# The low part of every third block of weights: a negated copy and an accumulating DMA in place of a subtraction

## The chip, the cores and the metric

The kernel runs on one NeuronCore of one Trainium2 chip. The metric is the device time of one execution in microseconds (us). The engines are named TensorE (PE; its weight loads are PEld), VectorE (DVE), ScalarE (ACT), GpSimd (POOL) and SyncE (SP).

## The reference

One layer of a decoder trunk for 256 tokens of width 2048, in float32. The input is RMS-normalised and multiplied by one wide matrix, `w_in`. From its columns come four attention mixers (sparse with an indexer, forgetting, differential, dilated), each with four heads, and their gates. Each mixer's output is projected by `w_branch` and merged, and the sum is projected by `w_out`.

```python
h = rms_norm(x, norm_w)
p = h @ w_in
...
for b in range(N_BRANCHES):
    y = branches[b].reshape(bsz, seq, BRANCH_WIDTH).astype(x.dtype) * jax.nn.silu(z_parts[b])
    term = jax.nn.sigmoid(g_parts[b]) * (y @ w_branch[b])
    merged = term if merged is None else merged + term
return (x + merged @ w_out).astype(x.dtype)
```

The final output is one more RMS norm. Nearly all of the work is in the matrix products with the three weight matrices, about 177 MB of weights, each of which is read once.

## The kernel before, in words

**Products in two parts.** TensorE multiplies in a reduced float32 format (`F32R`). To keep float32 accuracy each operand is split in two: the high part is the value rounded to that format, and the low part is the value minus the high part. A product is the sum of three: high by high, high by low, low by high. The activations are split once; the weights are split as they come.

**Units.** The weights are cut into 169 units (class `Unit`). A unit is mostly four chunks of 128 rows by 512 columns, 1024 KB, and the products that use it. There are two forms. In a [column, token] unit (`T_units`, for q, k and the gate path z) the weights are the stationary operand: for each of 16 blocks there is one product with the high part (line 278, 512 columns of tokens in two parts) and one with the low part (line 283, 256 columns). In a [token, column] unit (`tok_units`, for v, the gates, `w_branch` and `w_out`) the activations are stationary and the weights stream: 24 products per unit, in triples (lines 273, 274, 275), of which the third streams the low part. The order of the units is written out at the end of `body`: the indexer's 8 units and a small one, then for each of the four mixers 16 units for q, k, z and v, 16 for gates and 4 for `w_branch`, and at the end 16 for `w_out`.

**Load and split.** `load` (line 118) brings a unit's weights to a tile `raw` by a DMA issued from SP; there are 4 such tiles. `split` has ScalarE copy `raw` to the high part `whi` (line 134) and VectorE subtract that from `raw` into the low part `wlo` (line 135). `whi` and `wlo` have three buffers each (`SPLIT + 1`), used in turn. The main loop (line 839) issues for unit i: the split of unit i+2, the load of unit i+6, the products of unit i, the evictions of its results (`post`), and then one step of each active thread (attention heads and other small work, which use all engines). The engines run their own instructions in this order. So the split of unit i+2 writes the buffers that unit i-1 has read.

**Other work on the queues.** GpSimd does the scaling by 1/rms of q, k and z (lines 334, 345), the merge's additions (line 658), small operations of the differential mixer (lines 605, 606), and a few DMAs, among them the loads of `xf` and `fw` for the end (lines 670, 672). ScalarE does half of the evictions, the exponentials and the sigmoids. SP issues only the loads and, at the end, the stores.

Of the kernel before, what the change touches and what calls it, by code (L numbers as in the profile page):

```python
# [11 lines left out]
F32 = mybir.dt.float32  # L12
F32R = mybir.dt.float32r
AF = mybir.ActivationFunctionType
ALU = mybir.AluOpType

P = 128
# [35 lines left out]
def shape_constants():  # L53
    """Rows: one-hot T5 bucket of each distance, causal mask, dilated multiplicity."""
    oh = np.zeros((NBUCKETS + 2, VLEN), np.float32)
    for i in range(VLEN):
        d = i - 127
        if d < 0:
            oh[NBUCKETS:, i] = NEG
            continue  # L60
        oh[bucket(d), i] = 1.0
        mult = int(d <= 128) + int(d % 4 == 0) + int(d % 16 == 0)
        oh[NBUCKETS + 1, i] = math.log(mult) if mult else NEG
    co = np.zeros((NBUCKETS + 2, 13), np.float32)
    co[NBUCKETS, 0:8] = 1.0
    co[NBUCKETS, 12] = 1.0
    co[NBUCKETS + 1, 8:12] = 1.0
    return oh, co


class Unit:
    """A block of weights (nk chunks of 128 rows by n columns) and the products that use it."""

    def __init__(self, src, k0, nk, c0, n, mm, post=(), need=(), start=()):
        self.src, self.k0, self.nk, self.c0, self.n = src, k0, nk, c0, n
        self.mm, self.post = mm, list(post)
        self.need, self.start = list(need), list(start)


@with_exitstack  # L80
def body(ctx: ExitStack, tc, x, norm_w, w_in, fox_b_f, lq1, lk1, lq2, lk2, subln_w,
         w_branch, w_out, rel_bias, final_w, oh, co, out):
    nc = tc.nc
    x = x[0]
# [20 lines left out]

# [1 line left out]
    def load(u, parts=1, part=None):  # L107
# [14 lines left out]
    def split(u, hi=None, lo=None, parts=1, part=None):  # L122
        if not part:
            if hi is None:
                hi = wp.tile([P, 2048], F32R, name="whi", tag="whi", bufs=SPLIT + 1)
                lo = wp.tile([P, 2048], F32R, name="wlo", tag="wlo", bufs=SPLIT + 1)
            n_ = u.nk * u.n
            u.hi = hi[:, :n_].rearrange("p (k n) -> p k n", k=u.nk)
            u.lo = lo[:, :n_].rearrange("p (k n) -> p k n", k=u.nk)
        step = u.nk // parts  # L130
        raw = u.raw[:, :u.nk * u.n].rearrange("p (k n) -> p k n", k=u.nk)
        for i in range(0, u.nk, step) if part is None else (part * step,):
            s_ = slice(i, i + step)
            nc.scalar.activation(u.hi[:, s_], raw[:, s_], AF.Copy)  # L134
            nc.vector.tensor_tensor(u.lo[:, s_], raw[:, s_], u.hi[:, s_].bitcast(F32),  # L135
                                    op=ALU.subtract)

# [1 line left out]
    nw = const.tile([16, P], F32, name="nw")  # L139
# [29 lines left out]

# [1 line left out]
    hT = big.tile([P, KC, 2, S], F32R, name="hT", tag="r1")  # L171
# [45 lines left out]

# [1 line left out]
    bias = at.tile([P, 13, S], F32, name="bias")  # L219
# [27 lines left out]

# [1 line left out]
    def h_act(k):  # L249
        return hT[:, k, 0], hT[:, k, 1]  # L250

    def tok_units(src, c0, act, nk, evict, name, n=512, need=(), start=()):
        """[token, column] tiles, activations stationary."""
        st = {}
        units = []
        for k0 in range(0, nk, 4):
            def mm(u, k0=k0):
                if k0 == 0:
                    st["ps"] = [main_ps(name) for _ in range(2)]
                for t in range(2):  # L260
                    tok_mm(st["ps"][t][:, :n], u, act, k0, nk, t)
            units.append(Unit(src, k0, 4, c0, n, mm))
        units[0].need += need
        units[-1].post.append(lambda: evict(st["ps"]))
        units[-1].start += start
        return units
# [19 lines left out]
    def T_units(c0, evict, name, start=(), ps_of=main_ps):  # L286
        """512 columns as four [column, token] tiles; each bank holds two halves to be added."""
        st = {}
        units = []
        for k0 in range(0, KC, 4):  # L290
            def mm(u, part=None, between=None, k0=k0):
                if k0 == 0 and not part:
                    st["ps"] = [ps_of(name) for _ in range(4)]
                ps = st["ps"]
                if part is None:
                    for j in range(4):
                        for k in range(4):
                            T_hi(ps[j], u, k0, j, k)
                            T_lo(ps[j], u, k0, j, k)
                else:  # L300
                    for f in (T_hi, T_lo):
                        for k in (2 * part, 2 * part + 1):
                            for j in range(4):
                                f(ps[j], u, k0, j, k)
                            if between is not None:
                                between()
                                between = None
            units.append(Unit(w_in, k0, 4, c0, 512, mm))
        units[-1].post.append(lambda: evict(st["ps"]))
        units[-1].start += start  # L310
        return units
# [45 lines left out]

# [1 line left out]
    ki_hi = at.tile([P, S], F32R, name="ki_hi")  # L359
# [15 lines left out]
    def misc_thread():  # L375
# [9 lines left out]
        for t in range(2):  # L385
# [3 lines left out]
                                           rst[:, t:t + 1], bf_sb, op0=ALU.mult, op1=ALU.add)  # L389
        # cumulative log forget gates, as rows: log sigmoid(f) = min(f, 0) - log(1 + exp(-|f|))  # L390
        fv = fl.rearrange("p t h -> p (t h)")
# [21 lines left out]
    def fox_bias(t, h):  # L413
        """Where the first branch's biases were."""
        return bias[:, h] if t else selb[h // 2][:, (h % 2) * P:(h % 2 + 1) * P]
# [18 lines left out]
    def ev_iq(ps, i):  # L434
        """Four chunks of two heads each; a head's high and low parts stacked on the partitions."""
        qf = big.tile([P, 4, S], F32, name="qf", tag="y")
        for j in range(4):
            add_halves(qf[:, j], ps[j])
        active.append(("", stack_thread(qf, i)))
# [47 lines left out]

# [1 line left out]
    # A head's logits: columns 0:128 the first query block, 128:384 the second.  # L489
    SL = (slice(0, 128), slice(128, 384))  # L490
# [8 lines left out]
    def softmax(ps, bias_of):  # L499
        """exp(logit - max) and its sums."""  # L500
        lg = at.tile([P, 384], F32, name="lg", tag="lg", bufs=3)
# [17 lines left out]
    def transposed(pr):  # L519
        """[key, query] pieces: keys 0:128 x queries 0:256, keys 128:256 x queries 128:256."""  # L520
        tp = att_ps("ptp")
        nc.tensor.transpose(tp[:, 0:128], pr[:, 0:128], ident)
        nc.tensor.transpose(tp[:, 128:256], pr[:, 128:256], ident)
        nc.tensor.transpose(tp[:, 256:384], pr[:, 256:384], ident)
        pt = at.tile([P, 384], F32, name="pt", tag="pt", bufs=2)
        nc.scalar.activation(pt, tp[:, :384], AF.Copy)
        return pt
# [5 lines left out]
    def put_y(h, o, scale=None):  # L533
        """o: [column, token]; the branch's product with its gate path, split."""
        yT = V["yT"]
# [82 lines left out]

# [1 line left out]
    V["g"] = {}  # L620
# [41 lines left out]

# [1 line left out]
    def open_final():  # L664
# [20 lines left out]
    def partial(t):  # L685
        """All of the mean square but its last piece, and epsilon."""
        part = V["mg"].tile([P, 1], F32, name="part", tag="part", bufs=2)
# [4 lines left out]
    def final(t, n, part):  # L692
        """1 / rms times the columns (all but the last n have final_w in them)."""
        xf, fs, fw = V["xf"], V["fs"], V["fw"]
# [23 lines left out]
    def out_units(n):  # L718
        if n < 3:
# [3 lines left out]
            return tok_units(w_out, n * 512, m_act, KC, ev, "ps_o")  # L723
        # the last columns: one token block after the other, the weights kept
        st = []
# [21 lines left out]

# [1 line left out]
    def att_threads(b, fn):  # L749
# [21 lines left out]

    # startup: x and the first weights by pairs of chunks, the tensor engine kept awake
    warm = att_ps("warm")
# [31 lines left out]

    # the first units by halves, x made ready one half ahead
    for p_ in range(2 * RAMP):
# [31 lines left out]
    for i in range(RAMP, len(units)):  # L839
        u = units[i]  # L840
# [45 lines left out]
```

## Time and profile before

| what | value |
|---|---|
| median of 2 runs | 999.6 us (999.59 to 999.6) |
| span of the profiled execution | 997.9 us, first to last instruction |
| around the span | 1.7 us between the median and this span |
| mean granted TensorE clock | 0.998 |
| bytes moved by DMA | 187.42 MB, 188 GB/s |

The profiled execution has no time of its own besides its span; the median of the runs stands beside it. Busy times are sums of instruction durations on an engine. The granted clock is a share of 2.4 GHz. Landing is the time from a DMA's issue to its completion.

### The profile page before, as it was taken

How to read it: one execution, taken by the hardware profiler on the slowest of the kernel's cores; microseconds unless marked ns; L12 is line 12 of the kernel's file. 1: busy time of each engine (PE TensorE's matmuls, PEld its weight loads, DVE VectorE, ACT ScalarE, POOL GpSimd, SP SyncE). 2: the span in 40 equal slices, each digit the busy share in tenths (PEclk: the TensorE clock that was granted, in tenths of full speed). 3: DMA queues.
4: the chain of work that ended last, by engine and by line, in shares of the span. 5: the costliest groups of instructions: out<-in, count | busy, mean ns of one | idle time of the engine just before them, and what ended most of it. 6: DMA issues, size and time to landing. Idle time of an engine off the chain costs nothing.

```text
span 997.9 us, 11965 instructions
## 1 busy us (share of the span) xinstructions
PE 989.2 (99%) x4935; PEld 833.2 (83%) x4935; DVE 559.9 (56%) x642; ACT 467.6 (47%) x502; POOL 92.5 (9%) x87
## 2 busy tenths in 40 slices
PE   9999999999999999999999999999999999999996
PEld 8888888888888888888888877888888888888886
DVE  5767777554556545545555455648454555366443
ACT  5764555543434355534343455643434454444441
POOL 2022010000001100002200000004000000031110
PEclk9999999999999999999999999999999999999999
DMA  9765555565656565556565645565565555855632
GB/s 322 225 212 201 196 173 170 170 207 174 227 175 205 169 199 181 169 170 206 178 204 170 206 133 168 169 193 186 172 202 185 178 173 187 310 196 169 194 102 85
DMA packets 97687, 187.42 MB, mean 188 GB/s; under 512 B 7507, under 2 KB 9717, under 8 KB 97248
## 3 DMA queue, kind: packets, MB, share of 16 engines
q1 hardware_dynamic: 96240, 181.06, 55.0%
q0 software_dynamic: 1360, 5.59, 1.5%
q8 instruction: 39, 0.64, 0.2%
q14 instruction: 16, 0.13, 0.0%
q10 hardware_dynamic: 32, 0.01, 0.0%
HBM read 184.52 MB, written 2.12 MB: 187 GB/s over the span
## 4 chain that ended last, share of the span: by engine, by line
PE 99%; issue 1%; ACT 0%; POOL 0%; DVE 0%; POOLq 0%; ACTq 0%
PE ps_g L273 12%; PE ps_g L275 12%; PE ps_g L274 12%; PE ps_q L278 6%; PE ps_k L278 6%; PE ps_z L278 6%; PE ps_z L283 3%; PE ps_q L283 3%; PE ps_k L283 3%; PE ps_iq L278 3%; PE ps_v L273 3%; PE ps_v L275 3%; PE ps_b L273 3%; PE ps_b L275 3%; PE ps_v L274 3%; PE ps_b L274 3%
## 5 line engine op out<-in xcount | busy, mean ns | idle before, releaser
L135 DVE TENSOR_TENSOR wlo<-raw,whi 128x2048 fp32r<-128x2048 f32 (+3 forms) x175 | 400.5, 2290 | 336.6 <-ACT whi L134 336.6
L134 ACT ACTIVATE whi<-raw 128x2048 fp32r<-128x2048 f32 (+3 forms) x175 | 321.6, 1841 | 273.2 <-issue 48.5
L273 PE MATMUL ps_g<-whi,hT 128*128 128x512 f32 x512 | 204.9, 400 | 0.0
L275 PE MATMUL ps_g<-wlo,hT 128*128 128x512 f32 x512 | 199.7, 390 | 0.0
L274 PE MATMUL ps_g<-whi,hT 128*128 128x512 f32 x512 | 199.7, 390 | 0.0
L273 PEld LDWEIGHTS ps_g<-whi,hT 128*128 128x128 f32 x512 | 96.2, 188 | 21.7 <-issue 2.0
L275 PEld LDWEIGHTS ps_g<-wlo,hT 128*128 128x128 f32 x512 | 96.2, 188 | 20.6
L274 PEld LDWEIGHTS ps_g<-whi,hT 128*128 128x128 f32 x512 | 96.3, 188 | 19.0
L278 PE MATMUL ps_q<-hT,whi 128*128 128x512 f32 x256 | 91.0, 400 | 0.0
L278 PE MATMUL ps_k<-hT,whi 128*128 128x512 f32 x256 | 90.8, 399 | 0.0
L278 PE MATMUL ps_z<-hT,whi 128*128 128x512 f32 x256 | 90.7, 399 | 0.0
L283 PE MATMUL ps_z<-hT,wlo 128*128 128x256 f32 x256 | 71.9, 281 | 0.0
L283 PE MATMUL ps_k<-hT,wlo 128*128 128x256 f32 x256 | 71.9, 281 | 0.0
L283 PE MATMUL ps_q<-hT,wlo 128*128 128x256 f32 x256 | 71.9, 281 | 0.0
L278 PEld LDWEIGHTS ps_q<-hT,whi 128*128 128x128 f32 x256 | 48.1, 188 | 12.5 <-issue 0.6
L278 PEld LDWEIGHTS ps_z<-hT,whi 128*128 128x128 f32 x256 | 48.1, 188 | 11.8
L278 PEld LDWEIGHTS ps_k<-hT,whi 128*128 128x128 f32 x256 | 48.1, 188 | 11.9
L273 PE MATMUL ps_b<-whi,yT 128*128 128x512 f32 x128 | 49.9, 390 | 0.0
L273 PE MATMUL ps_v<-whi,hT 128*128 128x512 f32 x128 | 49.9, 390 | 0.0
L275 PE MATMUL ps_v<-wlo,hT 128*128 128x512 f32 x128 | 49.8, 389 | 0.0
L275 PE MATMUL ps_b<-wlo,yT 128*128 128x512 f32 x128 | 49.8, 389 | 0.0
L274 PE MATMUL ps_v<-whi,hT 128*128 128x512 f32 x128 | 49.8, 389 | 0.0
(208 smaller groups left out, 1269.6 us busy)
## 6 DMA issues: line engine op xcount, KB each, us to landing
raw<-in_w_in_dram SPq DMA_DIRECT2D x132, 1024.0 KB, 4.9
raw<-in_w_branch_dram SPq DMA_DIRECT2D x16, 1024.0 KB, 4.9
raw<-in_w_out_dram SPq DMA_DIRECT2D x16, 1024.0 KB, 5.0
raw<-in_w_in_dram SPq DMA_DIRECT2D x7, 512.0 KB, 10.6
xs<-in_x_dram SPq DMA_DIRECT2D x8, 256.0 KB, 8.1
xf<-in_x_dram POOLq DMA_DIRECT2D x2, 1024.0 KB, 8.7
bt<-vdr POOLq DMA_DIRECT2D x1, 1664.0 KB, 11.3
out_dram<-xf SPq DMA_DIRECT2D x5, 256.0 KB, 2.8
```

What stands on the lines that cost most here:

```text
L134: nc.scalar.activation(u.hi[:, s_], raw[:, s_], AF.Copy)
L135: nc.vector.tensor_tensor(u.lo[:, s_], raw[:, s_], u.hi[:, s_].bitcast(F32), op=ALU.subtract)
L273: nc.tensor.matmul(ps, ahi[:, ts_], u.hi[:, k, cols], start=first, stop=False)
L274: nc.tensor.matmul(ps, alo[:, ts_], u.hi[:, k, cols], start=False, stop=False)
L275: nc.tensor.matmul(ps, ahi[:, ts_], u.lo[:, k, cols], start=False, stop=last)
L278: nc.tensor.matmul(ps[:m], u.hi[:, k, j * P:j * P + m], hT[:, k0 + k].rearrange("p a s -> p (a s)"), start=k0 + k == 0, stop=False)
L283: nc.tensor.matmul(ps[:m, :S], u.lo[:, k, j * P:j * P + m], hT[:, k0 + k, 0], start=False, stop=k0 + k == KC - 1)
```

## The change

Before the startup, every third unit from number 24 on, up to the last four, is marked (`acc`). For a marked unit `split` does not use VectorE. ScalarE writes the high part as before, and then writes its negative to the low part's tile. GpSimd then issues a DMA that reads the unit's weights from memory a second time and adds them to that tile, so that the tile holds the weights minus the high part. The load to `raw` stays. Products, buffers, the order of units and everything else stay as they are. (The diff also drops comments, which are left out here.)

```diff
@@ class Unit
         self.need, self.start = list(need), list(start)
+        self.acc = False
...
@@ def split
         raw = u.raw[:, :u.nk * u.n].rearrange("p (k n) -> p k n", k=u.nk)
+        if u.acc:
+            nc.scalar.activation(u.hi, raw, AF.Copy)
+            nc.scalar.activation(u.lo, u.hi.bitcast(F32), AF.Copy, scale=-1.0)
+            nc.gpsimd.dma_start(u.lo, u.src[u.k0 * P:(u.k0 + u.nk) * P, u.c0:u.c0 + u.n]
+                                .rearrange("(k p) n -> p k n", p=P), accum_op=ALU.add)
+            return
         for i in range(0, u.nk, step) if part is None else (part * step,):
...
@@ the order of things
+    for u in units[24:-4:3]:
+        u.acc = u.n == 512
```

## Rows read from the trace of the kernel before

**Rows 1.** The page: busy us and share of engines; the clock and DMA in 40 slices.
```profile
PE 989.2 (99%) x4935; PEld 833.2 (83%) x4935; DVE 559.9 (56%) x642; ACT 467.6 (47%) x502; POOL 92.5 (9%) x87
...
PEclk9999999999999999999999999999999999999999
DMA  9765555565656565556565645565565555855632
```

**Rows 2.** The chain that ended last, by engine, from the page.
```profile
PE 99%; issue 1%; ACT 0%; POOL 0%; DVE 0%; POOLq 0%; ACTq 0%
```

**Rows 3.** Waits of TensorE's weight loads: who for whom, us, times, longest.
```profile
PEld warm L777 <- DVE ones L143: 1.1, 1, 1.1
...
PEld ps_o L275 <- DVE wlo L135: 0.2, 1, 0.2
```

**Rows 4.** Timeline of ScalarE: start us, us, instruction, [idle before]; around 310 and 680.
```profile
304.35 1.92 ACT L134 ACTIVATE whi<-raw 128x2048 fp32r<-128x2048 f32 x1 [3.34 <-PE ps_k L278]
...
315.67 1.92 ACT L134 ACTIVATE whi<-raw 128x2048 fp32r<-128x2048 f32 x1 [3.74 <-PE ps_k L278]
...
666.06 1.92 ACT L134 ACTIVATE whi<-raw 128x2048 fp32r<-128x2048 f32 x1 [3.52 <-PE ps_g L274]
...
672.83 1.91 ACT L134 ACTIVATE whi<-raw 128x2048 fp32r<-128x2048 f32 x1
...
682.59 1.92 ACT L134 ACTIVATE whi<-raw 128x2048 fp32r<-128x2048 f32 x1 [3.47 <-PE ps_b L274]
688.02 1.93 ACT L134 ACTIVATE whi<-raw 128x2048 fp32r<-128x2048 f32 x1 [3.52 <-PE ps_b L274]
```

**Rows 5.** Timeline of TensorE at the ends of two units of k.
```profile
304.15 0.28 PE L283 MATMUL ps_k<-hT,wlo 128*128 128x256 f32 x1
...
315.58 0.40 PE L278 MATMUL ps_k<-hT,whi 128*128 128x512 f32 x1
...
315.59 0.19 PEld L283 LDWEIGHTS ps_k<-hT,wlo 128*128 128x128 f32 x1
```

**Rows 6.** Timeline of VectorE: the subtraction after the high part of 304.35.
```profile
306.30 2.29 DVE L135 TENSOR_TENSOR wlo<-raw,whi 128x2048 fp32r<-128x2048 f32 x1 [0.95 <-ACT whi L134]
```

**Rows 7.** DMA issues: what, queue, count, KB each, median us to landing.
```profile
raw<-in_w_in_dram SPq DMA_DIRECT2D x132, 1024.0 KB, 4.9
...
xf<-in_x_dram POOLq DMA_DIRECT2D x2, 1024.0 KB, 8.7
bt<-vdr POOLq DMA_DIRECT2D x1, 1664.0 KB, 11.3
...
fw<-in_final_norm_w_dram POOLq DMA_DIRECT2D x1, 1024.0 KB, 12.4
...
ncb<-ncd POOLq DMA_DIRECT2D x1, 512.0 KB, 5.1
```

**Rows 8.** GpSimd's two DMAs of line 670: issue in ns, min/median/max, and landing.
```profile
L670 POOL DMA_DIRECT2D xf<-in_x_dram x2: 538/587/636, 849.0 to 849.6; - x2
...
DMA to landing us min/median/max: 7.6/8.7/9.8
```

**Rows 9.** Stretches: busy us of engines, clock, DMA share, GB/s; ordinary, then beside line 670.
```profile
299.00:321.00 22.00, 22.00 (x127) 19.07 (x126) 14.64 (x14) 8.80 (x8) 2.40 (x1) 1.00 0.55 189
...
851.00:863.00 12.00, 12.00 (x54) 9.95 (x53) 4.91 (x3) 5.91 (x5) 0.00 (x0) 1.00 1.01 403
```

**Rows 10.** Stretches at the run's end; the third figure from the right is the clock.
```profile
990.00:992.00 2.00, 0.28 (x3) 0.08 (x1) 0.64 (x2) 0.51 (x2) 0.33 (x1) 1.00 0.00 0
...
992.50:993.00 0.50, 0.00 (x0) 0.00 (x0) 0.50 (x3) 0.50 (x2) 0.00 (x0) 1.00 0.00 0
993.00:993.50 0.50, 0.00 (x0) 0.00 (x0) 0.41 (x2) 0.50 (x2) 0.00 (x0) 0.50 0.03 10
```

## The prediction

> **What bounds the kernel now.** I began with the page. TensorE is busy 989.2 of 997.9 us at full clock, while VectorE is at 56%, ScalarE at 47%, and the DMA engines are mostly five or six tenths busy [rows 1]. The chain that ended last is 99% TensorE [rows 2]. Next, who waits: of all weight loads, one waited 0.2 us for a low part, and none for anything else of the split [rows 3]. So nothing outside TensorE is worth time as long as the weights are ready. VectorE's subtraction, which the change removes, is hidden; removing it can earn 0.2 us. The whole question is whether the new way to the low part still fits in the time that TensorE leaves it.
>
> That time is read from the timeline. The high part of unit i+2 goes to the buffer that unit i-1 frees, so ScalarE starts it when unit i-1 reads its last high part. At 304.35 the copy to the high part starts, and the next but one follows at 315.67, two paces of 5.66 us [rows 4]; in a stretch of [token, column] units they stand 5.43 us apart (682.59, 688.02) [rows 4]. The unit after next begins with the product at 315.58, and its first low part is loaded as weights at 315.59 [rows 5]. So from the start of the high part to the first need of the low part there are 315.59 - 304.35 = 11.2 us. In the other kind of unit it is alike: two paces of 5.43 us, 10.9 us, to its first product, and the low part is first in its third, so a little more; I use 11.2 us for both. Before the change the chain is 1.92 us (ScalarE) and 2.29 us (VectorE, 306.30 to 308.59) [rows 4, 6]: 4.2 of 11.2 us are used, and 7 us are spare.
>
> **The change, part by part.** The slice [24:-4:3] of 169 units holds 47, all with 512 columns, none in the startup.
>
> VectorE loses 47 subtractions at 2.29 us, 108 us of its 560 [rows 1, 6]. Nothing waited for them, so this earns nothing. Had the cover been thin, it would show as waits for wlo, and there is the 0.2 us alone [rows 3].
>
> ScalarE gains 47 full-width copies with a scale of -1. The nearest row is its own copy of the same shape, 1.92 us [rows 4]; bounds 1.9 to 2.3 us (the subtraction's price). It adds 47 x 1.92 = 90 us to 468 us of busy time [rows 1], and this is no bound by itself. It does not wait further: the low part's old reader, the last product of unit i-1 (304.15), has read it by 304.5 [rows 5], before the high part is done at 306.27. Behind it on ScalarE stand the evictions of unit i, which can't start before about 5.5 us; the copy ends at 3.8 us. What is late is the start: where an eviction or a softmax is ahead, the high part starts late (672.83 where 666.06 + 5.43 = 671.5 was due, 1.3 us [rows 4]). I take 0.3 us as a mean, since about one unit in four follows an eviction; 0 and 1.3 are the ends.
>
> GpSimd gains 47 DMA issues at 0.54 to 0.64 us [rows 8], 28 us in all. The wait for the copy blocks its queue: behind it are the merge's additions, the scaling of q, k and the gate, and the tiny operations of the differential mixer. These belong to the threads and evictions of unit i, due a unit later than the copy ends, so I price this at nothing, at most one issue (0.6 us) where one of them is on a head's chain.
>
> SP's loads go on, since the high part still comes from raw: no load is saved. A load behind such a unit is released by the high part and not by the subtraction, some 2.3 us earlier; loads run four units ahead, so it gains nothing, but it falls together with the new DMA.
>
> The new DMA is the term that decides. It moves 1024 KB again, 47 x 1.05 = 49 MB more. At what time must it have landed? The low copy ends 3.84 us after the start, plus 0.1 us: from issue to landing there are 11.2 - 3.9 = 7.3 us, less the 0.3 us of late starts, 7.0 us. No row shows an accumulating DMA. Plain rows: 4.9 us from SP, 8.7 us median from GpSimd (7.6 and 9.8, two beside one another), 12.4 us for a third one behind them, 11.3 us for 1664 KB, and 5.1 us for half the size [rows 7, 8]. Bounds: 4.9 us below (it is as fast as SP's), 17.4 us above (twice 8.7, all of it doubled). Of these I take GpSimd's own 8.7 us for 1024 KB, as the same size from the same queue beside the same loads, and add what it has to read besides: an addition needs the old contents of the destination, another 1.05 MB. At the 403 GB/s that the busy engines moved in that stretch [rows 9] this is 2.6 us. Landing: 11.3 us. The DMA engines have the room, at a 0.55 share in an ordinary stretch [rows 9], but the loads stand in the same engines, which is in the 8.7 already.
>
> The Trainium skill, "Collectives: The Full Stack", section "The bandwidth ceiling: the fold count and why AG ≠ RS ≠ AR", says that an addition in a DMA has to read two sources, and that this, not the adding, halves its rate. By GpSimd's row alone, as a plain transfer, the sum would be 1080 us (the second case below); with the page's doubled reading it is the forecast's. No run so far shows which.
>
> Stall: 11.3 - 7.0 = 4.3 us per unit. The buffers rotate by three and the changed units come every third, so each changed unit takes the buffer that the changed unit before it left. The period is one unit plus the longer of two units and this chain; the two units between are ready early but don't shorten it. Nothing is made up for, and nothing adds up: 47 x 4.3 = 202 us.
>
> Then the clock. At the end of the run TensorE is busy for 0.28 us after 990.0 and then no more; the clock is still 1.00 until 993.0 and 0.50 from there [rows 10]: after an idle stretch of under 3 us it fell to 1.2 GHz. A stall of 4.3 us is longer than that. What low clock costs a unit is shown by no row: none (back at once) up to 5.5 us (the whole unit at half speed). I take a quarter, 1.4 us, since only a part of the stalls need end in a fall and the unit's products would bring the clock back: 47 x 1.4 = 66 us.
>
> Sum: the profiled execution spans 997.9 us; the two timed runs have a median of 999.6, 1.7 us more, which the change leaves alone. 997.9 + 202 + 66 + 1.7 = 1268 us.
>
> **The rivals.** (a) The transfer is hidden: it lands within 7.0 us. For it: SP's 4.9 us and the 5.1 us for half the size [rows 7]; a lone transfer need not share with two others as the 8.7 did. Against it: the least that GpSimd's 1024 KB took is 7.6 us [rows 8]. TensorE then doesn't stall, the clock stays, and the time is 1000 us. It decides from a landing of 7.0 us; up to 7.4 us (0.4 x 47 = 19 us) it is still within 2%. This is the case on the other side, not slower. Nothing makes it faster by 2%, as no wait of TensorE goes.
> (b) The destination's reading runs along for nothing: it lands in 8.7 us, the stall is 1.7 us, too short for the clock to fall. 999.6 + 47 x 1.7 = 1080 us.
> (c) The whole of it doubles, 17.4 us: for it, rows of 2 KB with a read of two places each; against it, the engines' free 45%. 10.4 x 47 = 489, with the clock's 66: 1555 us.
> (d) As forecast, but the clock stays low through the unit: 47 x 5.5 = 259 in place of 66: 1460 us.
> That the change does nothing can't be: all 47 units pass through the split's new branch.
>
> **How the numbers follow.** Forecast 0.42 (landing 10 to 13 us, 1150 to 1400 us), (a) 0.09, (b) 0.20, (c) 0.22, (d) 0.07. A measurement tells about 2% from no change. Faster by over 2%: 0.01; within 2%: 0.09; slower: 0.90. The range leaves out (a) and the upper end of (c) and goes from 1065 to 1500 us.
>
> **What would show it.** Right: the weight loads (or products, where the low part streams) of every third unit wait for the DMA on wlo, about 47 times 4 us; TensorE's busy share falls to near 80%; the issue list has wlo from in_w_in at 10 to 13 us; L135 falls by 47; slices of PEclk below 9. A ScalarE near 44% and a VectorE near 36% of the span show that neither bounds. Wrong: no wait for wlo and a landing under 7 us (a); waits of under 2 us with a full clock (b); a landing above 15 us (c). Waits for whi, or of the products for raw, would mean that ScalarE or the loads, which I price at nothing, have become the bound. The period is wrong if the stall is not the same at each of the 47.

## The result and the profile after

The changed kernel takes 1120.4 us (1119.6 to 1121.2, 2 runs) where the kernel before took 999.6 us; the ratio is 1.1207 with a 95% interval of 1.1189 to 1.1225. It is slower by 121 us. The forecast was 1268 us, slower by 268: the direction and the mechanism came out, the size is less than half of it.

The page of the changed kernel: busy time of the engines, then the clock and the DMA engines in 40 slices, then two DMA queues (packets, MB, share of 16 engines).

```profile
span 1119.5 us, 12050 instructions
...
PE 1023.9 (91%) x4935; PEld 847.4 (76%) x4935; DVE 450.8 (40%) x595; ACT 556.3 (50%) x549; POOL 152.6 (14%) x134
...
PEclk9999999999999999999999999999999999998999
DMA  9765577778887876887879787788788869796651
...
q1 hardware_dynamic: 96240, 181.06, 48.1%
q0 software_dynamic: 26176, 54.87, 27.9%
...
DMA 25%; PE 17%; ACT 12%; issue 5%; DVE 1%; ACTq 0%; POOL 0%; POOLq 0%
```

Against [rows 1] and [rows 2] the reader sees three things. TensorE went from 99% to 91% of a longer span: 95.6 us idle where it was 8.7. The last fenced line is the chain that ended last: 99% TensorE before, now a mix in which the DMA has 25% and ScalarE 12%. The digits of PEclk hide the clock, since a slice is 28 us long; its mean fell from 0.998 to 0.976.

The waits of TensorE's weight loads, in the columns of [rows 3]:

```profile
PEld ps_g L282 <- DMA wlo<-in_w_in_dram: 41.3, 20, 3.2
PEld ps_v L282 <- DMA wlo<-in_w_in_dram: 18.5, 7, 4.7
PEld ps_q L290 <- DMA wlo<-in_w_in_dram: 13.1, 6, 2.7
PEld ps_o L282 <- DMA wlo<-in_w_out_dram: 11.8, 4, 4.6
PEld ps_k L290 <- DMA wlo<-in_w_in_dram: 8.2, 3, 3.2
PEld ps_b L282 <- DMA wlo<-in_w_branch_dram: 7.9, 4, 2.6
PEld ps_z L290 <- DMA wlo<-in_w_in_dram: 5.3, 3, 2.0
```

The counts add to 47, one for each changed unit, and the waits to 106 us, 2.26 us each. No weight load waits for `whi` or `raw`, so neither ScalarE nor the loads are what is late.

One such unit from start to end, in the timelines of ScalarE, GpSimd and the weight loads:

```profile
365.77 1.92 ACT L134 ACTIVATE whi<-raw 128x2048 fp32r<-128x2048 f32 x1 [5.34 <-PE ps_z L285]
367.72 1.92 ACT L135 ACTIVATE wlo<-whi 128x2048 fp32r<-128x2048 f32 x1
...
369.93 1.29 POOL L136 DMA_DIRECT2D wlo<-in_w_in_dram  x1 [13.62 <-ACT wlo L135]
...
378.57 0.19 PEld L282 LDWEIGHTS ps_v<-wlo,hT 128*128 128x128 f32 x1 [1.44 <-DMA wlo<-in_w_in_dram]
```

High part, negated copy, issue 0.3 us after the copy's end, and the first use of the low part 8.64 us after the issue. TensorE had come to that weight load 1.44 us earlier, at 377.13, which is 11.4 us after the high part's start: the deadline that [rows 4] and [rows 5] gave as 11.2 us. The issue list has the landing of the new DMAs, in the columns of [rows 7],

```profile
wlo<-in_w_in_dram POOLq DMA_DIRECT2D x39, 1024.0 KB, 8.8
```

and, from the view of their line, over all 47:

```profile
DMA to landing us min/median/max: 8.4/8.8/12.9
```

The clock shows in short stretches only. Around the longest stall (4.7 us, to 399.5), in the columns of [rows 9]:

```profile
396.00:398.00 2.00, 0.00 (x0) 0.00 (x0) 1.51 (x1) 0.46 (x1) 0.00 (x0) 1.00 1.06 307
398.00:400.00 2.00, 0.49 (x1) 0.49 (x2) 0.79 (x1) 0.00 (x0) 0.00 (x0) 0.89 0.92 305
400.00:402.00 2.00, 2.00 (x6) 1.52 (x6) 0.00 (x0) 0.00 (x0) 0.00 (x0) 0.50 0.84 266
402.00:404.00 2.00, 2.00 (x9) 1.59 (x8) 0.00 (x0) 0.30 (x1) 0.00 (x0) 0.76 0.68 262
404.00:406.00 2.00, 2.00 (x10) 1.65 (x9) 0.00 (x0) 0.39 (x1) 0.00 (x0) 1.00 0.00 0
```

The clock stays at 1.00 while TensorE idles, falls to 0.50 (1.2 GHz) near the stall's end and is back at 1.00 in the stretch from 404: 6 products in the stretch from 400 where 10 fit at full clock. In the whole run 14 of the 47 stalls go with such a fall, and the clock missing in them adds to 25.6 us. So the 121.6 us by which the span grew divide into about 26 us of low clock and 96 us of stall, 2.0 us a unit (a part of a weight load's wait lies beside the product that is still running). The page agrees: TensorE's idle time grew by 87 us, and its busy time by 35 us, most of which is the low clock's.

### The profile page after: what moved, and what is told of

It reads as the page before. It is cut to its first block, busy times and chain, and to the rows that moved or that the text cites. A ratio compares the mean times of both kernels' runs of the same rounds, so it can differ in the third digit from the quotient of the medians.

```text
span 1119.5 us, 12050 instructions
## 1 busy us (share of the span) xinstructions
PE 1023.9 (91%) x4935; PEld 847.4 (76%) x4935; DVE 450.8 (40%) x595; ACT 556.3 (50%) x549; POOL 152.6 (14%) x134
## 3 DMA queue, kind: packets, MB, share of 16 engines
q0 software_dynamic: 26176, 54.87, 27.9%
## 4 chain that ended last, share of the span: by engine, by line
DMA 25%; PE 17%; ACT 12%; issue 5%; DVE 1%; ACTq 0%; POOL 0%; POOLq 0%
DMA wlo<-in_w_in_dram 20%; ACT whi L134 5%; ACT wlo L135 5%; DMA wlo<-in_w_out_dram 3%; DMA wlo<-in_w_branch_dram 2%; PE ps_g L282 2%; PE ps_g L280 2%; PE ps_g L281 2%; PE ps_o L282 2%; PE ps_o L280 2%; PE ps_o L281 2%; PE ps_q L285 1%; PE ps_q L290 1%; ACT whi L141 1%; PE ps_k L285 1%
## 5 line engine op out<-in xcount | busy, mean ns | idle before, releaser
L142 DVE TENSOR_TENSOR wlo<-raw,whi 128x2048 fp32r<-128x2048 f32 (+3 forms) x128 | 287.6, 2249 | 364.1 <-ACT whi L141 364.0
L141 ACT ACTIVATE whi<-raw 128x2048 fp32r<-128x2048 f32 (+3 forms) x128 | 231.4, 1812 | 144.7 <-PE ps_g L281 35.8
L282 PE MATMUL ps_g<-wlo,hT 128*128 128x512 f32 x512 | 205.3, 401 | 32.7 <-DMA wlo<-in_w_in_dram 32.7
L280 PE MATMUL ps_g<-whi,hT 128*128 128x512 f32 x512 | 208.0, 406 | 0.0
L281 PE MATMUL ps_g<-whi,hT 128*128 128x512 f32 x512 | 202.7, 396 | 0.0
L134 ACT ACTIVATE whi<-raw 128x2048 fp32r<-128x2048 f32 x47 | 89.9, 1913 | 145.5 <-PE ps_g L281 27.5
L136 POOL DMA_DIRECT2D wlo<-in_w_in_dram x39 | 50.4, 1292 | 539.2 <-ACT wlo L135 417.2
L280 PEld LDWEIGHTS ps_g<-whi,hT 128*128 128x128 f32 x512 | 98.2, 192 | 21.8 <-issue 2.0
L281 PEld LDWEIGHTS ps_g<-whi,hT 128*128 128x128 f32 x512 | 98.2, 192 | 20.0
L135 ACT ACTIVATE wlo<-whi 128x2048 fp32r<-128x2048 f32 x47 | 90.1, 1917 | 1.5
L282 PE MATMUL ps_o<-wlo,mT 128*128 128x512 f32 (+1 forms) x132 | 51.1, 387 | 10.1 <-DMA wlo<-in_w_out_dram 10.1
L290 PEld LDWEIGHTS ps_q<-hT,wlo 128*128 128x128 f32 x256 | 49.9, 195 | 13.1 <-DMA wlo<-in_w_in_dram 13.1
```

Of the source, the lines that this page charges most:

```text
L134: nc.scalar.activation(u.hi, raw, AF.Copy)
L135: nc.scalar.activation(u.lo, u.hi.bitcast(F32), AF.Copy, scale=-1.0)
L136: nc.gpsimd.dma_start(u.lo, u.src[u.k0 * P:(u.k0 + u.nk) * P, u.c0:u.c0 + u.n] .rearrange("(k p) n -> p k n", p=P), accum_op=ALU.add)
L280: nc.tensor.matmul(ps, ahi[:, ts_], u.hi[:, k, cols], start=first, stop=False)
L281: nc.tensor.matmul(ps, alo[:, ts_], u.hi[:, k, cols], start=False, stop=False)
L282: nc.tensor.matmul(ps, ahi[:, ts_], u.lo[:, k, cols], start=False, stop=last)
```

## The experiments

Theory A: the loss is the low part coming too late, the landing against the 7 us that are spare, and the clock's falls after it. The rivals are named in the expectations. Each kernel is the changed one with the edit shown; two stand on an earlier experiment, as said there. The figures for a whole run stand beside runs of the kernel before on the same chip (999.7 to 1000.2 us).

**A plain copy in place of the addition** (the low part then holds the weights, and the addition is left out).

```diff
-                                .rearrange("(k p) n -> p k n", p=P), accum_op=ALU.add)
+                                .rearrange("(k p) n -> p k n", p=P))
```

> The same 47 DMAs at the same place and with the same waits, but as plain copies without the addition (the low part then holds the weights themselves, so the low products are left out of what is computed as such). Theory A (an addition also reads the destination, and the forecast's error was to add that to rows that were already crowded): a plain copy lands in 5.5 to 6.2 us, inside the 7 us that are spare, TensorE does not stall, 1000 to 1003 us. Theory B (8.8 us is what GpSimd's queue takes for 1024 KB with or without an addition): landing stays at 8.5 to 9 us and the time at 1120 us. Theory C (the extra traffic slows the loads): above 1050 us, with waits on raw or whi.

1002.0 us, ratio 1.0023 (1.0013 to 1.0034). Its queue and the new DMAs on the page:

```profile
q0 software_dynamic: 26176, 54.87, 17.2%
...
wlo<-in_w_in_dram POOLq DMA_DIRECT2D x39, 1024.0 KB, 5.4
```

and their issue on GpSimd, from the view of the line, in ns (min/median/max):

```profile
L136 POOL DMA_DIRECT2D wlo<-in_w_in_dram x39: 740/765/832, 147.9 to 862.4; - x39
```

Theory A holds, and B and C fall. A plain 1024 KB from the same queue at the same place lands in 5.4 us in the median, within the spare time; the addition makes it 8.8. A load close by lengthens the plain one too: one that was issued at 407.15, about 2 us behind two loads of SP's, landed after 9.1 us. The bytes in the queue's row are the same, 54.87 MB, but not the engines' time: 17.2% of 1000.2 us is 172 us, and 27.9% of 1119.5 us is 312 us. Without the 15 us of the queue's other DMAs (1.5% of 997.9 us on the page of before) that is 3.3 us of all 16 engines for a plain 1.05 MB and 6.3 us for an added one. The issue takes 1.29 us in place of 0.77.

**The low products last.** In the marked units all products with the high part come before those with the low part (`tok_mm`, not shown, then issues only the one or the other).

```diff
-                for t in range(2):
-                    tok_mm(st["ps"][t][:, :n], u, act, k0, nk, t)
+                for part in (("hi", "lo") if u.acc else ("both",)):
+                    for t in range(2):
+                        tok_mm(st["ps"][t][:, :n], u, act, k0, nk, t, part=part)
...
-                    for j in range(4):
-                        for k in range(4):
-                            T_hi(ps[j], u, k0, j, k)
-                            T_lo(ps[j], u, k0, j, k)
+                    for fs_ in (((T_hi,), (T_lo,)) if u.acc else ((T_hi, T_lo),)):
+                        for j in range(4):
+                            for k in range(4):
+                                for f in fs_:
+                                    f(ps[j], u, k0, j, k)
```

> In the 47 units the products with the high part come first and those with the low part last, so the low part is needed 3.2 to 3.8 us later; nothing else differs. Theory A (the whole loss is the low part coming 2 us after its time): 43 of 47 stalls of 0.8 to 3.2 us go, the clock stays at 1.00, 1000 to 1005 us, with the landing still at 8.8 us. Theory C (traffic or ScalarE's copy costs time by itself): 1050 us or more.

1001.7 us, ratio 1.0017 (1.0006 to 1.0029), clock 0.998. Busy engines and the new DMAs of this kernel:

```profile
PE 988.5 (99%) x4935; PEld 832.0 (83%) x4935; DVE 450.1 (45%) x595; ACT 557.0 (56%) x549; POOL 153.9 (15%) x134
...
wlo<-in_w_in_dram POOLq DMA_DIRECT2D x39, 1024.0 KB, 10.3
```

They land later than in the changed kernel, 10.3 us in place of the 8.8 us expected. I put that down to DMA engines that are denser in use where nothing stalls (the two large queues have 83% of the span here, 76% in the changed kernel); no run shows it apart. And yet all but 2 us of the loss is gone, by an order of products alone. Everything else of the change, the traffic, the copy and the issue, costs at most these 2 us together; some short waits for `wlo` (2.7 us of weight loads) are still among them.

**Pairs of neighbours.** The same number of units but one, two in every six.

```diff
-    for u in units[24:-4:3]:
-        u.acc = u.n == 512
+    for i, u in enumerate(units[24:-4]):
+        u.acc = u.n == 512 and i % 6 < 2
```

> 48 units instead of 47, but in pairs of neighbours, two in every six instead of one in every three. Theory A: the second of a pair has its chain started before the first one's stall, so that stall is spare time for it; 24 stalls of 2 us and 7 clock falls, 24 x 2.6 = 62 us, 1062 us, up to 1090 us if the two DMAs lengthen one another where they overlap. Theory C (a price per DMA, wherever it stands): 48 x 2.57 = 123 us, 1123 us.

1157.6 us, ratio 1.1575 (1.1552 to 1.1598): worse than either expectation. The clock is lower, too: 0.954, which by (0.998 - 0.954) x 1154.7 is some 51 us of the loss. One pair in the timelines of GpSimd and of the weight loads:

```profile
194.03 1.27 POOL L136 DMA_DIRECT2D wlo<-in_w_in_dram  x1 [37.67 <-DVE sm L566]
200.36 1.29 POOL L136 DMA_DIRECT2D wlo<-in_w_in_dram  x1 [5.05 <-ACT wlo L135]
...
202.49 0.19 PEld L282 LDWEIGHTS ps_g<-wlo,hT 128*128 128x128 f32 x1 [2.56 <-DMA wlo<-in_w_in_dram]
...
211.28 0.19 PEld L282 LDWEIGHTS ps_g<-wlo,hT 128*128 128x128 f32 x1 [2.81 <-DMA wlo<-in_w_in_dram]
```

and the stretches between them, whose last two columns are the DMA engines' share and GB/s:

```profile
196.00:198.00 2.00, 2.00 (x10) 1.66 (x9) 0.00 (x0) 2.00 (x2) 0.00 (x0) 1.00 1.04 159
198.00:200.00 2.00, 2.00 (x13) 1.66 (x12) 0.00 (x0) 1.97 (x3) 0.00 (x0) 1.00 1.13 206
```

The low part of the first is used 8.5 us after its issue, that of the second 10.9 us. So it is in 23 of the 24 pairs: the second is issued some 5 to 7 us behind and lands after 11 to 14.6 us. The pair that is left shows the other side:

```profile
681.04 1.27 POOL L136 DMA_DIRECT2D wlo<-in_w_in_dram  x1 [38.79 <-ACT wlo L135]
689.66 1.28 POOL L136 DMA_DIRECT2D wlo<-in_w_in_dram  x1 [7.34 <-ACT wlo L135]
```

Its second was issued 8.6 us behind, when the first had landed, and took 8.4 us. My reasoning that the first stall is spare time for the second left out that one accumulating DMA fills the engines: at a share of 1.04 the counter shows 159 GB/s, where plain transfers at that share moved 403 [rows 9].

**Pairs with plain copies** (the pairs above, with the addition left out as in the first experiment).

```diff
-                                .rearrange("(k p) n -> p k n", p=P), accum_op=ALU.add)
+                                .rearrange("(k p) n -> p k n", p=P))
```

> The pairs of neighbours again, 48 units, but with plain copies (the low part then holds the weights, so what is added is left out). In the accumulating pairs the first of two landed after 8.4 to 9.5 us mostly and the second, issued some 6 us later, after 11 to 14 us. Theory E (the second meets the first in the 16 engines, each addition taking 6 us of all of them): a plain copy takes half, the second lands within 7 us, no stall beyond some tenths, 1000 to 1006 us. Theory F (the second is late by what ScalarE has ahead of it, two extra copies in a row beside evictions, whatever the DMA does): landing short but stalls of 1 us and more at the second of each pair, 1030 us and above.

1006.3 us, ratio 1.0056 (1.0036 to 1.0075), on another chip, where the kernel before took 1000.1 us. Twelve stalls are left with 8.9 us together, the landing is 5.6 us in the median:

```profile
DMA to landing us min/median/max: 5.1/5.6/8.8
```

ScalarE's order is the same as in the pairs before, and 151 us are gone. So the second DMA of a pair was late by the first one's, not by ScalarE (theory F): a plain copy has mostly landed when the second is issued, an added one has not. Whether the second waits in the shared engines or only behind the first in GpSimd's queue is not told apart by these runs.

**The copy alone.** ScalarE's negated copy stays, VectorE adds the weights, no DMA.

```diff
-            nc.gpsimd.dma_start(u.lo, u.src[u.k0 * P:(u.k0 + u.nk) * P, u.c0:u.c0 + u.n]
-                                .rearrange("(k p) n -> p k n", p=P), accum_op=ALU.add)
+            nc.vector.tensor_tensor(u.lo, raw, u.lo.bitcast(F32), op=ALU.add)
```

> ScalarE writes the negated high part in the 47 units as in the change, but VectorE adds the weights and there is no DMA. Chain 1.9 + 1.9 + 2.3 = 6.1 us of 11.2. Theory A: no stall, 999 to 1001 us. Theory D (ScalarE's extra copy delays its evictions and through them TensorE): 47 x 0.5 to 1 us, 1020 to 1045 us.

1004.6 us, ratio 1.0042 (1.0026 to 1.0058), between the two expectations and near A. The one new wait of the weight loads is small:

```profile
PEld ps_z L284 <- DVE qk L323: 3.7, 3, 1.2
```

Three times VectorE reads the results of k late, and with them the banks come free late for z. With VectorE busy for these units, the longer chain is not quite free, 4 us; that VectorE has this time back with the DMA in its place is argued from its busy time, not shown apart.

**The stalls filled with products.** Seven products with an all-zero stationary operand ahead of the first low one.

```diff
+FILL_N = 7
...
             nc.tensor.matmul(ps, alo[:, ts_], u.hi[:, k, cols], start=False, stop=False)
+            if u.acc and k == 0 and t == 0:
+                for _ in range(FILL_N):
+                    nc.tensor.matmul(ps, zero, u.hi[:, k, cols], start=False, stop=False)
...
                             T_hi(ps[j], u, k0, j, k)
+                            if u.acc and j == 0 and k == 0:
+                                for _ in range(FILL_N):
+                                    nc.tensor.matmul(ps[j], zero,
+                                                     hT[:, k0 + k].rearrange("p a s -> p (a s)"),
+                                                     start=False, stop=False)
                             T_lo(ps[j], u, k0, j, k)
```

> In the 47 units TensorE gets 7 more products with an all-zero stationary operand (they add zero to the sums) just ahead of the first low one, 7 x 0.23 = 1.6 us in the place where it stalls. Theory A with the clock as a loss of its own (in the changed kernel 14 stalls of 2.25 us or more were followed by a fall, which cost about 26 us together): the rest of the stalls is mostly under 1.2 us, only the four of 3.8 to 4.7 us can still let it fall, so 26 x 10/14 = 18 us come back: 1100 to 1105 us with the clock above 0.99. Rival (the clock costs nothing here, the longer products are only drawn out by the late operands): 1120 us or a little more.

**The changed kernel once more**, beside it, with no edit.

> The changed kernel itself once more, beside the one with the filled stalls. All theories: 1120 us, 47 stalls of 2.0 to 2.3 us in the mean.

With the filled stalls 1088.2 us, ratio 1.0895 (1.0876 to 1.0913); the changed kernel beside it 1099.9 us, ratio 1.1005 (1.0967 to 1.1043). More work for TensorE, 329 products, made it 12 us faster in the median. The two profiled executions span 1102.5 and 1085.0 us, 17.5 us apart, and the clock went from 0.979 to 0.997. So the clock is a loss of its own: (0.997 - 0.979) x 1102.5 = 20 us. The four runs of the unedited kernel fit: those at a clock of 0.979 and 0.980 took 1104.2 and 1103.2 us, the two at 0.986 took 1096.6 and 1096.4 us. That 17.5 and not 20 came back I put down to the stalls that are shorter than the filling; no run shows that apart.

The second figure was not expected: the same kernel is 20 us faster here than in the first measurement. The new DMAs' landing in this run is

```profile
wlo<-in_w_in_dram POOLq DMA_DIRECT2D x39, 1024.0 KB, 8.5
```

0.3 us less, and 47 x 0.3 = 14 us; the waits for `wlo` add to 93 us in place of 106, and 11 stalls go with a fall of the clock in place of 14. Why the DMAs land sooner stays open. A kernel that waits for a latency moves with it, while the kernel before took 999.6 and 999.7 us in the two measurements. The other experiments are therefore read against the kernel before, and by their own landings.

**Every sixth unit.**

```diff
-    for u in units[24:-4:3]:
+    for u in units[24:-4:6]:
```

> Every sixth unit instead of every third, 24 units, so no two of the DMAs can meet. Theory A (a stall of its own for each unit, no carrying over, 121/47 = 2.57 us with the clock's part): 24 x 2.57 = 62 us, 1062 us. Theory E (the pairs showed it: accumulating DMAs fill the 16 engines, and the loads between them pay too, so that the loss grows faster than the count): below 1050 us, with a landing under 8.5 us.

1061.9 us, ratio 1.0623 (1.0567 to 1.0679), as theory A has it; the landing is 8.5 us as with every third:

```profile
wlo<-in_w_in_dram POOLq DMA_DIRECT2D x18, 1024.0 KB, 8.5
```

By the profiled spans a unit costs (1055.3 - 997.9) / 24 = 2.4 us here and (1102.5 - 997.9) / 47 = 2.2 us with every third, on the same chip; by the medians it is 2.6 and 2.1 us (two runs here, 10 us apart). The loss does not grow faster than the count, so theory E falls at this density: the price is each unit's own, and with two units between them the DMAs don't meet. That it is a little higher here stays open.

**Low products last, every second unit** (the edit is against the kernel with the low products last).

```diff
-    for u in units[24:-4:3]:
+    for u in units[24:-4:2]:
```

> The kernel with the low products last, but for every second unit, 71 units. Each accumulating DMA took 6.1 us of all 16 engines there and the loads 526 us in all: 71 x 6.1 + 526 = 959 us of engine time, nearly the whole span. Theory E (engine time is the next bound): landing well above 12 us, stalls come back, 1030 to 1100 us. Theory A alone (only the lateness counts, and it is covered): 1000 to 1010 us.

1027.6 us, ratio 1.0280 (1.0233 to 1.0326). The landing of this kernel's new DMAs:

```profile
DMA to landing us min/median/max: 8.3/9.5/16.0
```

and a long stretch of it, in the columns of [rows 9]:

```profile
150.00:950.00 800.00, 785.67 (x3767) 651.93 (x3766) 268.98 (x387) 485.38 (x440) 157.07 (x114) 1.00 1.02 271
```

The DMA engines' share is 1.02 over this stretch, and stalls are back, 24.9 us in 22 places. The median landing stayed below the 12 us that theory E expected. Where TensorE stalls, the DMA landed after 8.4 to 12.4 us (once 16.0, just behind the loads of `xf` and `fw`), and the low part was wanted 7.9 to 11 us after the issue. The direction is E's: past every third unit the change costs time again, 28 us. That the full engines are the reason is argued, not shown: the median landing is shorter here than with every third unit (10.3 us).

No version beat the kernel before; TensorE's own work stands at 989 us in it, and nothing here takes any of that away.

## Why the prediction was wrong in size

**The deadline was right.** 11.2 us from the high part's start to the first use, 3.9 us for copy and hand-over, 7.0 us to land in after the late starts: measured 11.2, 4.2 and 7.0 us in the mean of all 47 units. The order by three buffers was right, too: 47 stalls, nothing made up for, and nearly the same price per unit at every sixth. The prediction's sign that the period is wrong, stalls that are not the same, did appear: they last from 0.8 to 4.7 us. But the period is not what spreads them: the landings go from 8.4 to 12.9 us, and the time left for them from 5.2 to 9.3 us. The longest stall (4.7 us) had a landing of 11.3 us with 6.6 us left.

**The landing was mis-sized, and this is the step that failed.** The prediction took 8.7 us, GpSimd's row for 1024 KB, and added 2.6 us for reading the destination: 11.3 us. It measured 8.8 us in the median and 9.2 in the mean. The addition's part was near enough: 8.8 - 5.4 = 3.4 us. The base was wrong. The 8.7 us came from two transfers beside one another with a third behind them, in a stretch where the engines' share was 1.01 [rows 9]; the new DMAs have no other transfer of their queue beside them, and a plain one at their place takes 5.4 us. The prediction knew that the row was crowded ("beside one another") and named it in case (a), but in the sum it took the crowding for the ordinary loads' contention. A load close by does lengthen a transfer (the 9.1 us above), but the 5.4 us were measured beside the ordinary loads; that the rest of the 8.7 was the row's own neighbours is argued, since no run issues that transfer alone. The row nearest by conditions was the 512 KB one (5.1 us) or SP's 4.9 us [rows 7], not the row nearest by size and queue. With the mean landing, 9.2 - 7.0 = 2.2 us a unit, the sum would have had 104 us of waiting, against 106 measured, of which some 96 lengthened the run. In place of 202 us of stall that is 106 of the 147 us by which the forecast was too high.

The Trainium skill ("Collectives: The Full Stack", section "The bandwidth ceiling: the fold count and why AG ≠ RS ≠ AR") says of the adding step of a collective's ring that it reads two sources and so runs at half the rate of a copy. The trace agrees in engine time, 6.3 us for an added 1.05 MB and 3.3 us for a plain one; the landing, which holds more than engine time, grew from 5.4 to 8.8 us.

**The clock was mis-sized as well.** 66 us were put down, a quarter of a slow unit for each stall; it was 26 us, 14 falls at 1.8 us: 33 of the 47 stalls, 2.0 us in the mean where 4.3 were forecast, left the clock at 1.00. This is the other 40 of the 147 us. Yet case (b) was wrong to say that stalls of 1.7 us in the mean leave the clock alone: the stalls spread, and falls went with waits of 2.25 to 4.7 us.

**The rivals.** (a) is what happens without the addition, and with the low products last: not slower, as it said. (b) came nearest in time (1080 us) by a landing of 8.7 us, but by luck: its reason, that reading the destination is free, is wrong, since the addition costs 3.4 us; two errors cancelled. (c) and (d) did not occur.

**What was costed at nothing.** The subtraction's going earned nothing (rightly: with the stall covered the time is still 1001.7 us, not under 999.6). ScalarE's copy, GpSimd's issues and the doubled reading of 49 MB together cost at most 2 us once the lateness is covered; the issue is twice as long as the 0.64 us assumed, which is inside the landing.

## What to carry to other kernels

When work is moved to a DMA, first write down the deadline by the buffers' rotation, then the latency of one such transfer alone, and only then its bandwidth; a row of a transfer that stood beside others is no estimate for one that stands alone. A transfer that adds is two transfers in engine time, though the byte count shows one. If the operand comes late by a little, look whether the order of the products can put its use last before looking for buffers: here that left 2 us of a loss of 100 to 121 us.

## What the runs showed of the hardware that was not expected

An accumulating DMA of 1024 KB from GpSimd: issue 1.29 us (plain 0.77), landing 8.5 to 8.8 us in the median beside the ordinary loads (plain 5.4), 10.3 us where nothing stalls, 6.3 us of 16 engines (plain 3.3), with the same bytes in the queue's row. With two of them issued 6 us apart the second lands after 11 to 14 us.

TensorE's clock fell to 1.2 GHz with stalls as short as 2.25 us of a weight load's wait (the one that ended at 575.8), but not with every longer one (2.71 us at 462.2 and 3.22 us at 817.3 left it at 1.00), and each of 14 falls cost about 1.8 us. With products of an all-zero stationary operand in the stalls it did not fall (mean clock 0.997).
